# Half of an encoder's input projection as seven block products per pair of tiles, with the mixer's work put in another order

## The chip, the core and the metric

The kernel runs on one core of a Trainium2 chip. The metric is the device time of one execution in microseconds (us); of several runs the median counts. The core has five engines with instruction queues of their own: TensorE (PE, matrix products, results in PSUM banks), VectorE (DVE), ScalarE (ACT), GpSimd (POOL) and SyncE (SP, which here issues transfers). Each works through its queue in order and waits on semaphores for others.

## The reference

Two layers of a hybrid encoder on 1040 rows (16 learned tokens and 1024 inputs) of 1024 channels. Cut to what matters:

```
proj = rmsnorm(x) @ w_in                    # q, k, v, z, b, a, sc_b, sc_c, sc_h
q, k, v = silu(conv3(qkv));  q, k = l2norm(q), l2norm(k)
# per direction, 4 heads of 128, chunks: A = I + strict(beta k k^T * decay)
v_new = u - w @ S;  o = (q*exp(G)) @ S + attn @ v_new
S     = S * exp(G_last) + k_dec^T @ v_new   # the scan over the chunks
o = rmsnorm(o_fwd + o_bwd) * silu(z)
y = sc_b * conv3(sc_c * sc_h)
x = x + concat(o, y) @ w_out
x = x + (silu(h @ w_gate) * (h @ w_up)) @ w_down,   h = rmsnorm(x)
```

A final rmsnorm ends it. u and w come from a triangular solve with A in each chunk.

## The kernel before, in words

Everything lies transposed: 128 channels on the partitions, the 1040 rows along the free axis. Data are fp32; an operand of a dense product is split into a high and a low part (`split_scaled` L176, `wsplit` L124: high part by ACT, L130, low part by POOL or DVE, L131), and each k-step of a dense tile is three matmuls, wh·xh, wh·xl, wl·xh (L157, L158, L159 in `dense`, L146). A tile of the input projection (`inproj`, L290) is 128 output channels: 8 k-steps x 3 matmuls x 3 chunks of 348, 346 and 346 columns, 72 matmuls. In the last layer the gate tiles and the outer factors of the short convolution leave out the 16 tokens and have two chunks of 512.

A layer has four stretches. (1) The mixer's projection, 28 tiles: q 0 to 3, k 4 to 7, v 8 to 11, the gates z 12 to 15 and short convolution 16 to 27 (three tiles for each of four groups). The keys come first, then the queries. Each goes through a convolution of width 3 (`conv`, one ACT and two DVE instructions, L309 and L310), and q and k are normalised (`normalise`, L406) with lengths summed on PE. `k_out` (L418) transposes the keys and copies them by ACT (L426); `chunk_p` (L442) forms key products with their decay; `chunk_a` (L481) those of queries and keys. (2) In each chunk a triangular block is inverted: `substitute` runs 31 DVE steps for each direction, `invert` (L527) puts blocks together on PE and ACT. (3) The scan: `scan_step` (L769) per direction and chunk of 128 rows, nine steps each way. In a step, for four heads: ks = k·S (L792), r by DVE (L795), q·S (L802), its scaled copy qs by ACT (L804), vr (L807), vs by ACT (L810), vn by ACT (L812), then su (L816) for the new state S (DVE, L836) and po (L828, L830) for the output. q·S, vr and po share a PSUM bank of their direction, ks and su another. Once both directions have passed a chunk, `finalize` (L849) normalises its output by ACT and DVE, transposes it on PE (L870) and multiplies by the gate (L871). (4) The output projection (`out_part`, L941) and the feed-forward part, whose products are already done by the scheme of Strassen and Winograd: for four blocks A11 to A22 of weights, sums S1 to S4 of them, and sums T1 to T4 of the data, seven products instead of eight give the four blocks of the result (`prod` L1055, matmuls L1060 to L1062; the down projection L1426 to L1428). The S1 sums of the down projection (`s_under`, `s_sum`, adds at L1151) are made during the gate and up rows.

The order of the work comes from a scheduler that takes the recorded instructions by priority and data: `at_prio` sets the running priority, `mmp` holds a low one for dense matmuls that may fill gaps, `evp` one for evacuations of PSUM, and `jobs`, `jobs2` and `jobs3` are lists from which one small job each is taken after each dense chunk (the end of `dense`). From the values on, all dense tiles take the low priority: 4 value, 4 gate and 12 short-convolution tiles and the lower half of the output projection lie as fill under the second substitution, the inverses and the scan.

Of the kernel before, what the change touches and what calls it, by code (L numbers as in the profile page):

```python
# [15 lines left out]
KT = 8  # L16
# [26 lines left out]
def trunk(ctx: ExitStack, tc: tile.TileContext, xT, w_in, w_ba, w_out, w_gu, w_dn,  # L43
# [188 lines left out]
    for m in range(KT):  # L232
        cs = FULL if m == 0 else [(0, L)]
        for (n0, n1) in cs:
            dma(hv[m][:, n0:n1], xT[m][:, n0:n1])
            if n0 == 0 and m == 0:
                pre[4] = wload(w_in[0, 4], KT)
        for (n0, n1) in cs:
            lasts.append(split_scaled(hv[m][:, n0:n1], par[:, P_N1 + m:P_N1 + m + 1], x[m][0][:, n0:n1], x[m][1][:, n0:n1]))
        if m == 3:  # L240
            pre[5] = wload(w_in[0, 5], KT)
# [37 lines left out]
    hsrc = xT  # L279
    for l in range(DEPTH):  # L280
# [47 lines left out]
        gt = big("P0")  # L328
        wr = gt[:, 3, 0:128].rearrange("p (k m) -> p k m", k=8)
        wb = big("P1", F32R)[:, 0, 0:256].rearrange("p (k m) -> p k m", k=8)  # L330

        def gate_weights():
            dma(wr, w_ba[l])
            act(out=wb[:, :, 0:16], in_=wr, func=AF.Copy)
            tt(out=wb[:, :, 16:32], in0=wr, in1=wb[:, :, 0:16].bitcast(F32), op=ALU.subtract)

        def gates():
            bat = gt[:, 0, :]
# [18 lines left out]
            scr = gt[:, 1, :]  # L357
# [34 lines left out]
            grows = gt[0:72, 2, 0:128]  # L392
# [9 lines left out]


        kq = {"q": big(Y[0][1]), "k": big(Y[0][0])}
        QT, KTt = kq["q"], kq["k"]
        def normalise(dst, l2, r):  # L406

            r4 = row(Y[1] + "f")[:, 0:260]
            act(out=r4, in_=l2[:, 0:260], func=AF.Sqrt, scale=1.0, bias=epsc)
            nc.vector.reciprocal(out=r4, in_=r4)  # L410
            for h in range(H):
                qdma(rnd[r + h].rearrange("(a c) -> a c", a=4), r4.rearrange("(a b) c -> a b c", b=32)[:, h, :])
            for h in range(H):
                bc = c4k("bc")
                qdma(bc, rnd[r + h].partition_broadcast(128))
                tt(out=dst[:, h, :], in0=dst[:, h, :], in1=bc, op=ALU.mult)

        def k_out(c):  # L418
# [4 lines left out]
            for h in range(H):  # L423
                nc.tensor.transpose(ps[0:n, h * 128:(h + 1) * 128], KTt[:, h, s0:s0 + n], ident)
            kt = t2k("kt")
            act(out=kt[0:n].rearrange("p a b -> p (a b)"), in_=ps[0:n], func=AF.Copy)  # L426
            adma(vkd[c, 0:n, 1, :], kt[0:n].rearrange("p a b -> p (a b)"))
# [14 lines left out]
        def chunk_p(c):  # L442
# [8 lines left out]
            for h in range(H):  # L451
                mm(kk[0:n, h, 0:n], KTt[:, h, s0:s0 + n], KTt[:, h, s0:s0 + n], start=True, stop=True)
# [28 lines left out]
        def chunk_a(c):  # L481
# [3 lines left out]
            low(lambda: [mm(qk[0:n, h, 0:n], KTt[:, h, s0:s0 + n], QT[:, h, s0:s0 + n], start=True, stop=True) for h in range(H)])  # L485
# [41 lines left out]
        def invert(d):  # L527
# [19 lines left out]
            def first():  # L547
                for qs in halves:
                    ps = fb(32)
                    low(lambda: [mm(ps[B[s], q - qs.start, :], P_[B[f], q, B[s]], XB[B[f], q, :], start=True, stop=True, skip_group_check=True)  # L550
                                 for q in range(qs.start, qs.stop) for (f, s) in pairs])
# [3 lines left out]
            def second():  # L555
                for qs in halves:
                    ps = fb(32)
                    low(lambda: [mm(ps[B[f], q - qs.start, :], QS[B[s], q, :], P_[B[s], q, B[s]], start=True, stop=True, skip_group_check=True)
                                 for q in range(qs.start, qs.stop) for (f, s) in pairs])
# [3 lines left out]
            def third():  # L563
                f, s = pairs[0]
                fo, so = 32 * (f % 2), 32 * (s % 2)
                for qs in halves:
                    ps = fb(32)
                    low(lambda: [mm(ps[B[s], q - qs.start, :], P_[B[s], q, B[s]], QS[B[s], q, :], start=True, stop=True) for q in range(qs.start, qs.stop)])
# [8 lines left out]
            def fourth(qh):  # L577
                ps = fb(64)
                low(lambda: [mm(ps[S_, q, :], P_[F_, 8 * qh + q, S_], X64[F_, 8 * qh + q, :], start=True, stop=True) for q in range(8)])
                act(out=X64[S_, 8 * qh:8 * qh + 8, :], in_=ps[S_], func=AF.Copy, scale=-1.0)  # L580

            def fifth(qh):
                ps = fb(64)
                low(lambda: [mm(ps[F_, q, :], X64[S_, 8 * qh + q, :], P_[S_, 8 * qh + q, S_], start=True, stop=True) for q in range(8)])
# [6 lines left out]
        def sums(which, q, sq_):  # L591

            if which not in l2s:
                l2s[which] = bank("f")
            for j, (n0, n1) in enumerate([(260 * j, 260 * j + 260) for j in range(4)]):
                mm(l2s[which][32 * j:32 * j + 32, :n1 - n0], sel[:, 3 - q:35 - q], sq_[:, n0:n1], start=(q == 0), stop=(q == 3), skip_group_check=True)
            if q == 3 and which == "k":
                normalise(KTt, l2s["k"], 4)
            elif q == 3:
# [26 lines left out]
        seq = (4, 5, 6, 7, 0, 1, 2, 3)  # L626
        for pos, i in enumerate(seq):
            hh = pos % 4
            if pos == 2:
                gate_weights()  # L630
                evp[0] = base - 60000
            lov[0] = pos > 3
            t = trow()
            late = pos < (2, 1)[l]
            inproj(i, to_row_late(t) if late else to_row(t), pfirst if l == 0 and pos == 1 else None)
            if late:
                tt(out=t, in0=t, in1=rstd, op=ALU.mult)
            dst = (QT if i < 4 else KTt)[:, hh, :]
            if l == 0 and pos == 0:
                pre[seq[2]] = wload(w_in[l, seq[2]], KT)  # L640
            conv(t, dst, P_CV + 3 * i, whi_done[0] if l == 0 and pos == 0 else None)
            if i >= 4:
                lengths("k", hh, dst, t)
            if pos == 2:
                g, negG, nGb, negE, gl, bkd = gates()
            nxt = seq[pos + 1] if pos < 7 else 8
            if nxt not in pre:
                pre[nxt] = wload(w_in[l, nxt], KT)
            if pos == 3:
                jobs.append(None)  # L650
                jobs.extend([lambda c=c: k_out(c) for c in range(9)])
                jobs2.extend([None, None] + [lambda c=c: chunk_p(c) for c in range(9)])

        for hh in range(4):
            lengths("q", hh, QT[:, hh, :], c4k("sq"))
        qs_ = jobs[-4:]
        del jobs[-4:]
        jobs.extend([None, None, None, lambda: [f() for f in qs_]])
        sub_start()
        substitute(0)  # L660

# [3 lines left out]

        def z_tile(m):
            t = trow()
            inproj(12 + m, to_row(t), chunks=ochunks)
            t = t[:, o0:L]
            act(out=t, in_=t, func=AF.Silu)  # L670
            nc.gpsimd.tensor_scalar(out=t, in0=t, scalar1=pcol(P_DN), scalar2=1.0, op0=ALU.mult, op1=ALU.mult)
            dma(szd[m][:, o0:L], t)


        def low(f):

            here = tc.cur_priority
            at_prio(mmp[0])
            f()
            mmp[0] = tc.cur_priority  # L680
            at_prio(here)

        def v_store(i, v, c0):

            ps = pa()
            if c0 == 0:
                low(lambda: nc.tensor.transpose(ps[0:16, 0:128], v[:, 0:16], ident))
                vm = t2k("vm")[0:16, 0, :]
                here = tc.cur_priority
                at_prio(evp[0])  # L690
                nc.vector.tensor_copy(vm, ps[0:16, 0:128])
                evp[0] = tc.cur_priority
                at_prio(here)
                dma(vkd[0, 0:16, 0, i * 128:(i + 1) * 128], vm)
            else:
                vt = v[:, 16 + 128 * (c0 - 1):16 + 128 * (c0 + 3)]
                for c in range(4):
# [871 lines left out]
```

## Time and profile before

| | |
|---|---|
| median of three runs | 2561.62 us (2559.81 to 2562.78) |
| the profiled execution | 2561.09 us |
| its span | 2558.7 us |
| mean granted clock of TensorE | 0.995 |
| TensorE, VectorE, ScalarE, GpSimd busy | 97%, 64%, 42%, 45% of the span |
| layer 0: mixer, feed-forward, down | 0 to 603, 603 to 1073, 1073 to 1256 us |
| layer 1: mixer, feed-forward, down | 1256 to 1872, 1872 to 2316, 2316 to 2499 us |

Rows of the windows read: from and to in us, the length, then for each engine its busy time and (with x) its instructions, the granted clock, the share of busy DMA and GB/s. Rows of the timeline read: start, length, engine, line, operation, output and inputs, shape, count, and in brackets how long the engine had been idle and for what. A group of instructions reads: busy time in all and mean of one in ns, then the idle time just before them and what ended it. A row of waits reads: who waited for whom, us in total, times, the longest.

### The profile page before, as it was taken

Reading aid. Unit: us, or ns where it says so; the run is one execution under the profiler, and the core shown is the slowest. Engines: PE = TensorE matmul, PEld = TensorE weight load, DVE = VectorE, ACT = ScalarE, POOL = GpSimd, SP = SyncE. Lnnn points to the kernel's source line nnn. Section 1 sums busy time; section 2 is a strip of 40 time slices with the busy share of each in tenths; the row PEclk is TensorE's granted clock in tenths of the full one; section 3 lists DMA queues with packets and bytes.
Section 4 is the critical chain, followed back from the end, with each engine's and each line's share of the span. In section 5 each row is a group of like instructions: output and inputs, shape, how many; then the busy total and the mean of one; then the engine's idle time right before and its main releaser. Section 6 shows DMA issues by size and latency. Waiting matters only on the chain. (4 is left out here: it accounts for less than half of the span.)

```text
span 2558.7 us, 45283 instructions
## 1 busy us (share of the span) xinstructions
PE 2494.0 (97%) x17508; PEld 2280.6 (89%) x17508; DVE 1641.7 (64%) x2442; ACT 1070.0 (42%) x2053; POOL 1157.3 (45%) x885
## 2 busy tenths in 40 slices
PE   8999999999999999999999999999989999999998
PEld 6989999998899999999999988998967778887787
DVE  4689233748766666778556882236687776768764
ACT  5664233535233333444445742335442333334444
POOL 1141212525666666655320313123456676675662
PEclk9999999999999999999999999999999999999999
DMA  3444354624432222574224534445343322228641
GB/s 128 139 154 150 119 158 129 200 80 126 136 102 88 89 90 83 195 228 144 92 92 132 164 126 140 133 136 202 118 128 119 112 87 95 91 86 272 190 121 67
DMA packets 199532, 335.28 MB, mean 131 GB/s; under 512 B 23404, under 2 KB 85668, under 8 KB 199316
## 3 DMA queue, kind: packets, MB, share of 16 engines
q1 hardware_dynamic: 171204, 293.84, 35.4%
q10 hardware_dynamic: 25936, 34.19, 4.3%
q0 software_dynamic: 2176, 4.36, 0.5%
q8 instruction: 137, 2.24, 0.4%
q14 instruction: 79, 0.65, 0.1%
HBM read 250.31 MB, written 81.99 MB: 130 GB/s over the span
## 5 line engine op out<-in xcount | busy, mean ns | idle before, releaser
L131 POOL TENSOR_TENSOR wlo<-raw,whi 128x512 fp32r<-128x512 f32 x132 | 175.1, 1329 | 638.0 <-ACT whi L130 523.8
L157 PE MATMUL pacc<-a,whi 128*128 128x346 f32 (+1 forms) x808 | 264.1, 330 | 9.3 <-ACT whi L130 6.4
L159 PE MATMUL pacc<-a,wlo 128*128 128x346 f32 (+1 forms) x808 | 262.5, 326 | 0.6 <-DVE wlo L131 0.4
L157 PE MATMUL pacc<-b,whi 128*128 128x346 f32 (+2 forms) x672 | 233.9, 349 | 1.8 <-ACT b L900 1.8
L159 PE MATMUL pacc<-b,wlo 128*128 128x346 f32 (+2 forms) x672 | 233.0, 348 | 0.1
L158 PE MATMUL pacc<-a,whi 128*128 128x346 f32 (+1 forms) x688 | 225.8, 328 | 0.9 <-DVE a L901 0.9
L130 ACT ACTIVATE whi<-raw 128x512 fp32r<-128x512 f32 x168 | 105.3, 630 | 231.0 <-PE pacc L158 116.5
L158 PE MATMUL pacc<-b,whi 128*128 128x346 f32 (+2 forms) x580 | 200.4, 346 | 0.0
L1043 POOL TENSOR_TENSOR wlo<-rw,whi 128x512 fp32r<-128x512 f32 x92 | 134.6, 1465 | 72.8 <-ACT whi L1042 71.5
L157 PEld LDWEIGHTS pacc<-a,whi 128*128 128x128 f32 x808 | 152.8, 190 | 13.8 <-ACT whi L130 7.9
L159 PEld LDWEIGHTS pacc<-a,wlo 128*128 128x128 f32 x808 | 153.0, 190 | 1.9 <-DVE wlo L131 0.5
L157 PEld LDWEIGHTS pacc<-b,whi 128*128 128x128 f32 x672 | 126.8, 189 | 13.6 <-issue 3.1
L1043 POOL TENSOR_TENSOR a<-rw,a 128x512 fp32r<-128x512 f32 x64 | 105.3, 1646 | 68.2 <-ACT a L1042 65.5
L158 PEld LDWEIGHTS pacc<-a,whi 128*128 128x128 f32 x688 | 130.4, 190 | 5.4 <-issue 2.9
L159 PEld LDWEIGHTS pacc<-b,wlo 128*128 128x128 f32 x672 | 126.6, 189 | 9.2 <-issue 0.8
L1043 POOL TENSOR_TENSOR b<-rw,b 128x512 fp32r<-128x512 f32 x64 | 92.2, 1442 | 84.7 <-ACT b L1042 50.7
L1042 ACT ACTIVATE whi<-rw 128x512 fp32r<-128x512 f32 x92 | 57.8, 630 | 145.3 <-DVE rw L1288 85.0
L158 PEld LDWEIGHTS pacc<-b,whi 128*128 128x128 f32 x580 | 109.5, 189 | 6.9 <-issue 0.4
L1284 DVE TENSOR_TENSOR rw<-rw,rw 128x512 f32<-128x512 f32 x44 | 69.9, 1589 | 46.9 <-POOL wlo L1043 30.9
L1289 DVE TENSOR_TENSOR rw<-raw,rw 128x512 f32<-128x512 f32 x44 | 98.8, 2246 | 1.2
L1043 POOL TENSOR_TENSOR wlo<-raw,whi 128x512 fp32r<-128x512 f32 x50 | 77.9, 1560 | 33.6 <-ACT whi L1042 33.4
L1042 ACT ACTIVATE b<-rw 128x512 fp32r<-128x512 f32 x64 | 40.2, 630 | 123.1 <-PE pacc L1061 35.2
(973 smaller groups left out, 8417.4 us busy)
## 6 DMA issues: line engine op xcount, KB each, us to landing
raw<-in_w_in SPq DMA_DIRECT2D x112, 256.0 KB, 2.9
raw<-in_w_gu SPq DMA_DIRECT2D x104, 256.0 KB, 2.8
rw<-in_w_gu SPq DMA_DIRECT2D x88, 256.0 KB, 2.6
rw<-in_w_dn SPq DMA_DIRECT2D x94, 192.0 KB, 3.0
rec<-vkd SPq DMA_DIRECT2D x61, 256.0 KB, 3.3
raw<-in_w_out SPq DMA_DIRECT2D x48, 256.0 KB, 2.8
b<-ad SPq DMA_DIRECT2D x45, 260.0 KB, 3.0
a<-ad SPq DMA_DIRECT2D x45, 256.0 KB, 3.1
```

The source lines that it names most:

```text
L130: whi_done[0] = act(out=hi, in_=raw[:, 0:kk, :], func=AF.Copy)
L131: (tt if lov[0] else ptt)(out=lo, in0=raw[:, 0:kk, :], in1=hi.bitcast(F32), op=ALU.subtract)
L157: mm(ps[:, :n], wh, xh[:, n0:n1], start=(k == 0), stop=False)
L158: mm(ps[:, :n], wh, xl[:, n0:n1], start=False, stop=False)
L159: mm(ps[:, :n], wl, xh[:, n0:n1], start=False, stop=(k == K - 1))
L1042: act(out=hi, in_=src, func=AF.Copy)
L1043: ptt(out=lo, in0=src, in1=hi.bitcast(F32), op=ALU.subtract)
L1284: tt(out=s1t, in0=A21, in1=A22, op=ALU.add)
L1289: tt(out=A21, in0=A11, in1=A21, op=ALU.subtract)
```

## The change

**Products.** Of the 28 tiles of a layer 14 are taken in pairs: k 4 and 5, 6 and 7; v 8 and 9, 10 and 11; short convolution 16 and 17, 19 and 20, 18 and 21. A pair of tiles by two halves of the 8 k-steps is a 2 x 2 array of blocks, and the two halves of the 1040 columns make the data one; seven block products replace eight. `p_loads` fetches the blocks, `p_op` makes the sums S1 to S4 on DVE and splits them (ACT, POOL) three products ahead, `p_product` does the matmuls (two halves of 260 columns, four k-steps, three matmuls each: 168 in a pair) and adds the results up on DVE. `t_sums` and `t_part` make the data's T1 to T4, once per layer.

```diff
+        PAIRS = [("k", 4, 5), ("k", 6, 7), ("v", 8, 9), ("v", 10, 11), ("sc", 16, 17), ("sc", 19, 20), ("out", 18, 21)]
+        def t_sums(k):
+            w0, w1 = pcol(P_N1 + k), pcol(P_N1 + 4 + k)
+            b11, b12, b21, b22 = (h[:, k, HT * z:HT * z + HT] for h in (hA, hB) for z in (0, 1))
+            act(out=b12, in_=b12, func=AF.Copy, scale=w0)
+            stt(out=b11, in0=b11, scalar=npar[:, k:k + 1], in1=b12, op0=ALU.mult, op1=ALU.add)
...
+        def p_op(n):
+            p, i = divmod(n, 7)
...
+            elif i == 1:
+                r = st["S1"] = rw("ck2")
+                tt(out=r, in0=A21, in1=A22, op=ALU.add)
...
+            act(out=hi, in_=r, func=AF.Copy)
+            ptt(out=lo, in0=r, in1=hi.bitcast(F32), op=ALU.subtract)
...
+        def p_product(n):
...
+                    mm(ps, wh[:, k, :], xh, start=i < 3 and k == 0, stop=False, skip_group_check=True)
+                    mm(ps, wh[:, k, :], xl, start=False, stop=False, skip_group_check=True)
+                    mm(ps, wl[:, k, :], xh, start=False, stop=k == 3, skip_group_check=True)
...
+                if i == 0:
+                    act(out=u0, in_=ps, func=AF.Copy)
+                elif i == 5:
+                    tt(out=g0, in0=ps, in1=r0, op=ALU.mult)
+                else:
+                    to, by = {1: (u1, u0), 2: (g1, u0), 3: (g1, g1), 4: (u1, u1), 6: (u0, u0)}[i]
+                    tt(out=to, in0=ps, in1=by, op=ALU.add)
```

**Order of the mixer.** The four z tiles now come first, then the pairs, then the four query tiles, dense. Key products (`chunk_p`) are jobs under the first two query tiles; the first substitution is recorded behind them. The inverses, `chunk_a` and the second substitution follow at the plain priority, no longer the low one. Keys and queries exchange their buffers, and keys are normalised by pairs of heads.

```diff
+        for n in range(NPR):
+            p_product(n)
+            if n + 3 < NPR:
+                p_op(n + 3)
...
+            if n % 7 == 6:
+                p_rows(n // 7)
...
+        for i in range(4):
+            lov[0] = i < 2
...
+            inproj(i, to_row(tq[i]))
...
+            if i == 1:
+                sub_start()
+                substitute(0)
...
+        for f in invert(0):
+            f()
+        for c in (0, 1, 8, 2, 7, 3, 6, 4, 5):
+            chunk_a(c)
+        substitute(1)
+        for f in invert(1):
+            f()
+        mmp[0] = base + 1000000
...
+        lov[0] = False
+        sc_tile(2)
+        y3 = sc_tile(3)
```

Only these six tiles and the lower half of the output projection are left as fill of low priority. On PE in layer 0 a piece of the scan stood like this before, late in the program (L816, L828 and L807 are products of the scan; L157 to L159 are a dense tile):

```order
L157 MATMUL pacc_3982<-a_3_74,whi_3976 128x348
L816 MATMUL pf_4253<-vv_4251,rec_4246 128x128 x4
L158 MATMUL pacc_3982<-a_4_75,whi_3976 128x348
L828 MATMUL pf_4254<-vv_4251,rec_4246 128x128 x4
L807 MATMUL pb_4256<-vv_4252,P_843 128x128 x4
L159 MATMUL pacc_3982<-a_3_74,wlo_3977 128x348
L157 MATMUL pacc_3982<-a_3_74,whi_3976 128x348
```

Now PE's order in layer 0's scan, from the last rows of the last fill on. L960 is vr, L969 su, L981 po, L945 ks and L955 q·S, all of the forward direction (`pf`):

```order
L157 MATMUL pacc_5938<-a_557_5526,whi_5904 128x346
L158 MATMUL pacc_5938<-a3f_5535,whi_5904 128x346
L159 MATMUL pacc_5938<-a_557_5526,wlo_5905 128x346
L960 MATMUL pf_4671<-vv_4668,P_2669 128x128 x4
L969 MATMUL pf_4670<-vv_4668,rec_4663 128x128 x4
L981 MATMUL pf_4671<-vv_4668,rec_4663 128x128 x4
L945 MATMUL pf_4670<-S_4664,b_140_1000 128x128 x4
L955 MATMUL pf_4671<-S_4664,b_351_2641 128x128 x4
L960 MATMUL pf_4671<-vv_4668,P_2669 128x128 x4
L969 MATMUL pf_4670<-vv_4668,rec_4663 128x128 x4
```

The dense rows between the groups of the scan are gone from here to the output projection: 52 groups follow each other, 45 of the scan and 7 of transposes. The whole scan has nine steps in each direction; this is the fifth to the ninth. Some groups on, the backward direction (`pb`) follows, with the transposes of `finalize` (L1023) ahead of its products:

```order
L1023 MATMUL pa_5116<-ident,b3f_4674 128x128 x4
L960 MATMUL pf_4671<-vv_4668,P_2669 128x128 x4
L981 MATMUL pf_4671<-vv_4668,rec_4663 128x128 x4
L955 MATMUL pb_4673<-S_4665,b_140_1000 128x128 x4
L1023 MATMUL pa_5175<-ident,b3f_4674 128x128 x4
L960 MATMUL pb_4673<-vv_4669,P_2670 128x128 x4
L969 MATMUL pb_4672<-vv_4669,rec_4663 128x128 x4
```

A transpose of the finished chunk stands ahead of L960 on PE, in both directions.

DVE's order around the end of the second pair of keys, in layer 0: L757 and L760 evacuate products, L766 scales, L310 and L311 are the convolution, L446 the normalisation of the first pair, L716 the sum S4 of the next pair's weights:

```order
L757 TENSOR_TENSOR b_143_1017<-pacc_1018,rstd_81 128x260
L757 TENSOR_TENSOR b_143_1017<-pacc_1032,rstd_81 128x260
L760 TENSOR_TENSOR b3f_1016<-pb_1099,b3f_1016 128x260
L760 TENSOR_TENSOR b3f_1016<-pb_1113,b3f_1016 128x260
L766 TENSOR_TENSOR b3f_1016<-b3f_1016,rstd_81 128x520
L310 SCALAR_TENSOR_TENSOR b_140_1000<-b_143_1017,par,b_140_1000 128x1039
L311 SCALAR_TENSOR_TENSOR b_140_1000<-b_143_1017,par,b_140_1000 128x1039
L310 SCALAR_TENSOR_TENSOR b_140_1000<-b3f_1016,par,b_140_1000 128x1039
L446 TENSOR_TENSOR b_140_1000<-b_140_1000,bc_1060 128x1040
L311 SCALAR_TENSOR_TENSOR b_140_1000<-b3f_1016,par,b_140_1000 128x1039
L716 TENSOR_TENSOR rw_1260<-raw_1164,rw_1260 128x512
```

The sum S4, which a product waits for, stands behind the five long rows of the convolution and the normalisation.

**Down sums.** `s_under` now only issues the loads for the S1 sums; the adds stand behind the last operation of the row:

```diff
-            s_under(f)
+            adds = s_under(f)
...
-            tt(out=uv, in0=uv, in1=gv, op=ALU.mult)
+            row_done = tt(out=uv, in0=uv, in1=gv, op=ALU.mult)
+            for to, r, o in adds:
+                after(tt(out=to, in0=r, in1=o, op=ALU.add), row_done if f < FT - 1 else row_before)
+            row_before = row_done
```

355 lines of the change are left out of this document (224 added, 131 removed).

## The prediction

> **What bounds the kernel now.** First the page: how much of the span TensorE works.
>
> ```profile
> span 2558.7 us, 45283 instructions
> PE 2494.0 (97%) x17508; PEld 2280.6 (89%) x17508; DVE 1641.7 (64%) x2442; ACT 1070.0 (42%) x2053; POOL 1157.3 (45%) x885
> ```
>
> TensorE idles 64.7 us in all. So time comes off almost only where matmul work comes off, and every wait that the change adds to PE is paid in full. Next, what a matmul costs, by its columns: a stretch of layer 0's down projection (260 columns) and one of layer 1's feed-forward part (512).
>
> ```profile
> 1100.00:1175.00 75.00, 74.73 (x625) 1.00 0.63 192
> 2050.00:2100.00 50.00, 50.00 (x217) 1.00 0.25 84
> ```
>
> 75.0/625 is 120.0 ns and 50.0/217 is 230.4 ns, start to start; a line through both gives 158.0 ns at the 346.7 columns that a third of 1040 has. Cost goes by columns, so cutting the multiplications pays if PE stays fed. Then the windows in which PE idles in the mixer, which the change rebuilds, and those of the feed-forward part, whose scheme of products the change copies into the mixer.
>
> ```profile
> 100.00:125.00 25.00, 23.58 (x156) 1.00 0.65 208
> 125.00:150.00 25.00, 21.61 (x157) 1.00 0.71 219
> 150.00:175.00 25.00, 24.57 (x167) 1.00 0.45 143
> 475.00:500.00 25.00, 22.31 (x157) 1.00 0.83 287
> 500.00:525.00 25.00, 24.41 (x153) 0.93 0.31 99
> 600.00:625.00 25.00, 19.44 (x142) 0.93 0.31 95
> 1750.00:1775.00 25.00, 22.99 (x121) 0.93 0.79 288
> ```
>
> ```profile
> 600.00:725.00 125.00, 112.19 (x897) 108.94 (x895) 98.39 (x123) 47.30 (x81) 75.19 (x47) 0.99 0.39 124
> 725.00:1075.00 350.00, 344.38 (x2840) 341.42 (x2841) 224.93 (x291) 118.83 (x213) 225.38 (x139) 1.00 0.29 97
> ```
>
> In the second table the third busy column is DVE's. With DVE busy 64% (224.93 of 350) the block products lose 1.6% of PE; in the first 125 us, at 79%, they lose 12.8 us.
>
> **Term 1, the products: -37 us.** A dense tile is 72 matmuls (8 k-steps, 3 products, 3 chunks). Layer 0 gives up 14 tiles, 1008 x 158.0 = 159.3 us; layer 1 gives up 12, 136.5 us, and two that have 48 matmuls of 512, 96 x 230.4 = 22.1 us. Fourteen pairs come in, each 7 products x 4 k-steps x 3 x 2 halves = 168 matmuls of 260 columns: 2352 x 120.0 = 282.2 us. That is 317.9 out, 282.2 in, -35.7; counting one or two fewer matmuls in each window, as those at its edges are counted whole, gives -37. I take -37.
>
> **Term 2, key transposes: -5 us.** The three windows of 100 to 175 lose 1.42, 3.39 and 0.43. What PE waits for there is mostly ScalarE's copy of transposed keys, with no other ready work behind it in PE's order:
>
> ```profile
> PE pa L424 <- ACT kt L426: 2.7, 2, 1.4
> ```
>
> After the change the k_out jobs start three products after the keys' second pair, one product between jobs, so the copy has some 3 us of matmuls over it. All 5.2 us could go; if not, 0.
>
> **Term 3, the down sums: -6 us.** Before, the adds for S1 float among the feed-forward rows, and DVE, which works in order, sits in front of them until their loads land; matmuls wait for the evacuations behind. The first two rows are DVE's waits, the next two PE's in 660 to 715, the last two PE's in 1940 to 1980.
>
> ```profile
>   DMA S<-in_w_dn: 15.4, 7
>   DMA rw<-in_w_dn: 5.9, 4
> ...
> PE pacc L1060 <- DVE a L1326: 1.4, 1, 1.4
> PE pf L1060 <- DVE c L1326: 1.4, 1, 1.4
> ...
> PE pf L1060 <- DVE b L1326: 2.0, 1, 2.0
> PE pa L1060 <- DVE c L1308: 1.2, 1, 1.2
> ```
>
> These four come to 6.0. After, each add stands behind the last operation of its row, a whole row of the loop after its loads were issued, so the loads are hidden. The adds remain and could fall badly: bounds 0 and -8.
>
> **Term 4, the scan's end: +26 us.** Before, 4 value, 4 gate and 12 short-convolution tiles and the lower half of the output projection lie between the scan's steps to the end. After, only 6 tiles and that half are left for it, and in PE's order they run out five steps of nine before the end of each direction. From there PE has 45 groups of state products and 7 of transposes in layer 0, 49 and 7 in layer 1, and nothing else. What one step costs without fill is read from the last backward steps before, which are nearly bare:
>
> ```profile
> 457.23 1.05 PE L792 MATMUL pf<-S,b 128*128 128x128 f32 x8
> 458.12 1.06 PE L802 MATMUL pf<-S,b 128*128 128x128 f32 x8
> ...
> 486.91 1.05 PE L807 MATMUL pb<-vv,P 128*128 128x128 f32 x8
> 488.44 0.73 PE L816 MATMUL pb<-vv,rec 128*128 128x128 f32 x4
> 489.61 0.63 PE L870 MATMUL pa<-ident,b3f 128*128 128x128 f32 x4 [0.44 <-DVE b3f L868]
> 490.07 0.61 PE L816 MATMUL pb<-vv,rec 128*128 128x128 f32 x4
> 492.05 1.16 PE L792 MATMUL pb<-S,b 128*128 128x128 f32 x8 [0.32 <-DVE S L836]
> 493.52 1.05 PE L802 MATMUL pb<-S,b 128*128 128x128 f32 x8
> 495.85 1.16 PE L807 MATMUL pb<-vv,P 128*128 128x128 f32 x8
> ...
> 488.00 1.15 ACT L810 ACTIVATE vv<-pb,bkd 128x128 f32<-128x128 f32 x4
> 494.67 1.12 ACT L804 ACTIVATE qs<-pb,negE 128x128 f32<-128x128 f32 x4
> ...
> 490.88 1.11 DVE L836 SCALAR_TENSOR_TENSOR S<-S,gl,pb 128x128 f32<-128x128 f32 x4
> ```
>
> From one L807 to the next is 8.94 us: the upper price of a bare step. A lower one chains the same rows without what stood between: L807 to L810 1.09, to L816 0.44, four heads of L816 0.89 (the spacing of 457.23 and 458.12), L836 to L792 1.17, L792 to L802 0.89, L802 to L804 1.15, L804 to L807 1.18, in all 6.8. I take 7.4, nearer the lower, since in the row's step dense evacuations stood in DVE's way that will not be there; the finalize transposes (L870) still will. In PE's order layer 0's end has 6 such steps, one in which both directions share (10 groups, 9 us), and some 6.5 us at the hand-over between the directions and at the run-out (estimated): 44.4 + 9 + 6.5 = 59.9, against 45 x 0.89 + 7 x 0.46 (489.61 to 490.07) = 43.3 at PE's own pace. Layer 1 has 5 single and 2 shared: 61.5 against 46.8. The excess is 31.3. What the scan's end loses today goes off it: 2.69 + 0.59 (475 to 525) + 2.01 (1750 to 1775) = 5.3. Net +26; at 6.8 it is +19, at 8.94 +43.
>
> **Term 5, the pairs' feeding: +10 us.** A pair takes PE 20.2 us. What DVE does in it, by rows of before:
>
> ```profile
> L1284 DVE TENSOR_TENSOR rw<-rw,rw 128x512 f32<-128x512 f32 x44 | 69.9, 1589 | 46.9 <-POOL wlo L1043 30.9
> L905 DVE TENSOR_TENSOR a<-pacc,a 128x260 f32<-128x260 f32 x20 | 8.3, 420 | 5.7 <-PE pacc L159 5.7
> L309 DVE SCALAR_TENSOR_TENSOR a<-a,par,a 128x1039 f32<-128x1039 f32 x14 | 19.4, 1386 | 10.3 <-ACT a L308 10.3
> ```
>
> Four sums of weights 4 x 1.59, twelve evacuations 12 x 0.42, four convolution steps 4 x 1.39, and about 0.7 for the half row's scaling (half of such a 1039): 17.7 us, 88% of 20.2. Key pairs add two normalisations. Weight splits have 3 buffers each, and S4's sum stands behind the convolution in DVE's order. The nearest row at that load is 600 to 725. Without its first 25 us (start-up) it loses 7.3 of 100, and 3% if the DMA waits of term 3 are taken out; 725 to 1075 loses 1.6%. On 282 us: 20, 8.5 and 4.5. I take 10, bounds 4 and 20. The Trainium skill, SBUF — State Buffer, section Who interferes with whom, says that a DVE operation with two SBUF inputs and a GpSimd operation that reads SBUF block each other for a whole instruction. The 1589 mean of L1284 fits that; by the rule the four sums could each wait a whole split on POOL, some 8 us for the four, and the term would be nearer 17.
>
> **Term 6, the start: +4 us.** The first evacuation stands at
>
> ```profile
> 29.98 1.37 DVE L301 COPY b<-pacc 128x348 f32<-128x348 f32 x3 [5.78 <-PE pacc L159]
> ```
>
> DVE had been idle 5.78 us before it. Ahead of this copy now stand 12 half-row steps (0.7 each) and five whole-row subtractions (about 1.3), some 15 us, of which the idle 5.78 and DVE's earlier waits for ScalarE's splits hide most. PE meets it only when its banks are full: 0 to 6, taken 4, in layer 0 alone; in layer 1 these sums lie under dense tiles.
>
> Substitution and inverses I cost at nothing: two query tiles, key products and two more dense tiles, about 50 us of PE by the order, lie over the first substitution. If that cover is short, PE idles once in each layer. Normalisation in pairs and the exchanged buffers add no PE work.
>
> **Sum.** -37 - 5 - 6 + 26 + 10 + 4 = -8 on the profiled execution's 2561.1 us (span 2558.7 and 2.4 around it), which is 0.5 below the median of 2561.6: 2554. A measurement of this kernel can tell about 0.2%, 5 us, from no change.
>
> **The rivals.** *Slower: the bare scan.* From row 2679 of the order on, every finalize transpose stands ahead of the next state product on PE and waits for a chain over DVE and ScalarE; the 0.44 before L870 shows it in small. The eleven single steps decide: each 1 us more costs 11 us, and at 8.1 us a step the whole gain is gone; at the measured 8.94, +43 in place of +26 makes 2570; at 11 us it is 2593. For it: 8.94 is measured, not worked out. Against: fill stood in that step's way. Chance 0.30.
>
> *The pairs starve* like the first feed-forward rows, 7%: +20 instead of +10, 2563. Against it: no DMA wait stands in DVE's order there. Chance 0.15.
>
> *The tail is hidden*: the directions run side by side, two steps in 9 us, which is PE's own pace, so that only the 6.5 us of each layer's hand-over, less today's 5.3, is left, +8, and the pairs lose their least: 2561 - 37 - 5 - 8 + 8 + 4 + 4 = 2527. Against it: three forward steps stand alone in the order. Chance 0.10.
>
> *The clock falls in the bare tail.* The granted clock is 0.93 in the windows around short idle (500 to 525, 600 to 625, 1750 to 1775), 1.00 in the other windows above: such gaps already cost about 0.07 x 25 = 1.8 us of clock each. Were PE at half pace through the tail, four groups on each step's path would take 0.89 more, 11 x 3.6 = +39: 2593. The Trainium skill, TensorE: Matmul & The Clock Gate, Part 1, has such a rule: the array is let down to half its clock after an idle window of about 3.4 us. The 0.93 agrees with one window at half pace. Against it: by the rows above no gap inside a step is over some 1.2 us. Chance 0.05.
>
> *The change does not do what it says*: the filler was needed, and what comes off the products goes back one for one into the scan; that is 2561. It lies between the first rival and the forecast, chance 0.05.
>
> **The numbers.** The forecast, 2536 to 2558, has 0.35 and is the likeliest. Faster than by 5 us: 0.30 of the forecast's, 0.10 of the hidden tail, 0.04 of the starved pairs' and 0.03 of the others, 0.47. Within 5: 0.17. Slower: 0.36, the bare scan, the clock and the upper end of the starved pairs. The range reaches from the hidden tail's 2527, a microsecond off, to the 2593 of the clock and of the 11 us step.
>
> **What would show it.** Right: windows of 25 us inside the pairs with some 205 matmuls and PE above 24; no L424 wait; no PE wait behind down sums; and after the last dense matmul of the scan two stretches of some 60 us in each layer in which PE is 70 to 75% busy. Wrong: those stretches at 80 us and more, or windows in the pairs with PE under 23, or PE waiting on the inverses.

## The result and the profile after

The changed kernel takes 2670.5 us (median of four runs, 2665.2 to 2678.8) against 2561.0 before: ratio 1.043, 95% interval 1.041 to 1.044. It is slower by 109 us, where 8 us less were forecast, and lies beyond the range. The profiled execution's span is 2669.6 us. In the experiments below one of four runs took 8097 us (the dense tiles) and one 11626 us (one small job at a time); the ratios leave these two out, the medians do not. The head of the changed kernel's page:

```profile
span 2669.6 us, 46699 instructions
PE 2513.2 (94%) x17892; PEld 2291.0 (86%) x17892; DVE 1786.6 (67%) x2626; ACT 1125.4 (42%) x2148; POOL 1279.9 (48%) x979
```

Two things are to be read from it. TensorE's idle time rose from 64.7 to 156.4 us, 92 us more. And its busy time rose by 19.2 us, though by the forecast's first term some 37 us of matmul work were taken out. The mean granted clock is 0.976 where it was 0.995: over the spans that is 64 against 13 us of clock not granted, about as much as those 19 and 37. So there are two losses, waits and a slower clock. In windows of 50 us all of the added idle time lies in the two mixers: 59 us from 0 to 600 where it was 16, and 52 us in layer 1 (1300 to 1950) where it was 4 (1250 to 1850). Windows of PE show where in them (from and to, length, busy and matmuls, granted clock). The first row is the start before the change. The others are of the changed kernel: the start, the pairs of layer 0, the pairs of layer 1, and the scan's two ends:

```profile
0.00:50.00 50.00, 42.72 (x258) 1.00 0.44 148
...
0.00:50.00 50.00, 38.82 (x234) 0.97 0.47 159
...
100.00:250.00 150.00, 135.67 (x1063) 0.94 0.26 83
1425.00:1575.00 150.00, 131.22 (x1020) 0.94 0.27 84
525.00:605.00 80.00, 59.09 (x393) 0.91 0.41 120
1850.00:1925.00 75.00, 52.65 (x354) 0.89 0.40 121
```

The pairs lose 14 and 19 us to waits and up to 9 us each to the clock (0.06 of 150). The two ends of the scan lose 21 and 22 us to waits and 7 and 8 us to the clock. The middle, substitution and inverses, was costed at nothing and loses too, 12.9 us of waits from 250 to 450 and 5.9 from 1650 to 1700. Two of layer 0's windows:

```profile
300.00:325.00 25.00, 23.43 (x166) 1.00 0.23 79
325.00:350.00 25.00, 19.68 (x114) 0.86 0.35 114
```

Next, some of the longest waits of PE in the whole program. Here L1023 is the transpose of a finalized chunk, L955 q S, L960 vr, L515 the product of queries and keys, L454 and L429 the transposes of keys and values, L628 the sums of lengths, and L302 the evacuation of the first tiles:

```profile
PE pa L1023 <- DVE a3f L1021: 8.5, 5, 5.0
PE pb L960 <- ACT qs L957: 8.2, 10, 2.1
PE pb L515 <- DVE dt L519: 8.1, 3, 4.0
PE pb L955 <- DVE b3f L1011: 6.7, 3, 4.9
...
PE pa L454 <- DVE a L446: 4.3, 1, 4.3
PE pf L628 <- ACT a L655: 4.2, 2, 2.2
PE pf L628 <- ACT b L655: 4.0, 3, 2.0
PE pa L429 <- ACT kt L456: 3.6, 3, 1.5
...
PE pacc L157 <- DVE b L302: 3.4, 1, 3.4
```

Before the change the waits ahead of the same operations were small: 3.9 us ahead of the key transposes (L424), 0.8 ahead of the transposes of finalized chunks (L870) and 0.7 ahead of the sums of lengths (L596). The bare forward step, taken from one L960 to the next in the timeline of layer 0's scan:

```profile
523.88 1.05 PE L960 MATMUL pf<-vv,P 128*128 128x128 f32 x8
...
531.21 1.16 PE L960 MATMUL pf<-vv,P 128*128 128x128 f32 x8 [1.23 <-ACT qs L957]
...
538.64 1.16 PE L960 MATMUL pf<-vv,P 128*128 128x128 f32 x8 [1.23 <-ACT qs L957]
```

It is 7.33 and 7.43 us; the forecast had 7.4. So the price of a bare step was right. The later steps are others. Two backward L960 stand at 566.87 and 584.03, 17.2 us apart, and the chain that ended last passes between them over these pieces (start, length, what):

```profile
572.89 1.98 PE pb L945 x8
...
574.87 0.87 PE pa L1023 x4
...
575.79 2.67 DMA b3f<-od
...
578.62 1.27 POOL b3f L1010
...
579.91 0.70 DVE b3f L1011
...
580.66 2.08 PE pb L955 x8
```

The transposes of one chunk free its buffer; only then the other direction's output of the next chunk is loaded into it, GpSimd subtracts, VectorE adds the product and so frees the PSUM bank, and only then q S of the next step can start. PE idles 4.94 us. Two such chains lie in this one step, since a forward chunk is finalized ahead of the backward one. `finalize` alternates between two halves of one tile, but here they behave as one buffer: the loads of 559.34, 566.45, 575.79 and 583.66 each start within 0.1 us of the end of the transposes of the chunk directly before. The q S that follows lasts 2.08 us where it lasts 1.16 in other steps: the clock is at half there, as the windows of 10 us show. It was so already in the group of 572.89 (1.98 us), behind a wait of 1.70 us:

```profile
570.00:580.00 10.00, 4.02 (x21) 0.82 0.40 131
580.00:590.00 10.00, 8.41 (x36) 0.50 0.14 33
590.00:600.00 10.00, 8.20 (x61) 1.00 0.38 105
```

### The profile page after: what moved, and what is told of

It is laid out like the page before. It is cut to its first block, busy times and chain, and to the rows that moved or that the text cites. A ratio compares the mean times of both kernels' runs of the same rounds, so it can differ in the third digit from the quotient of the medians.

```text
span 2669.6 us, 46699 instructions
## 1 busy us (share of the span) xinstructions
PE 2513.2 (94%) x17892; PEld 2291.0 (86%) x17892; DVE 1786.6 (67%) x2626; ACT 1125.4 (42%) x2148; POOL 1279.9 (48%) x979
## 4 chain that ended last, share of the span: by engine, by line
PE 65%; DVE 18%; issue 5%; DMA 5%; ACT 4%; POOL 2%; ACTq 0%; SPq 0%; DVEq 0%; POOLq 0%
PE pacc L157 4%; PE pacc L159 4%; PE pacc L158 4%; PE pacc L1213 3%; PE pacc L1215 3%; PE pacc L1214 3%; PE pb L1213 2%; PE pb L1214 2%; PE pb L1215 2%; PE pf L1215 2%; PE pf L1214 2%; PE pf L1213 2%; PE pacc L1584 2%; PE pacc L1586 2%; PE pacc L1585 2%
## 5 line engine op out<-in xcount | busy, mean ns | idle before, releaser
L724 POOL TENSOR_TENSOR wlo<-rw,whi 128x512 fp32r<-128x512 f32 x70 | 100.8, 1448 | 149.8 <-ACT whi L723 143.0
L1196 POOL TENSOR_TENSOR wlo<-rw,whi 128x512 fp32r<-128x512 f32 x92 | 130.9, 1423 | 80.0 <-ACT whi L1195 72.7
L157 PE MATMUL pacc<-a,whi 128*128 128x346 f32 (+1 forms) x472 | 154.4, 334 | 11.2 <-ACT whi L130 5.7
L159 PE MATMUL pacc<-a,wlo 128*128 128x346 f32 (+1 forms) x472 | 155.5, 331 | 2.2 <-POOL wlo L131 2.1
L158 PE MATMUL pacc<-a,whi 128*128 128x346 f32 (+1 forms) x394 | 131.8, 335 | 0.6 <-DVE a L178 0.3
L157 PE MATMUL pacc<-b,whi 128*128 128x512 f32 (+2 forms) x352 | 126.6, 361 | 1.8 <-DVE a L757 1.5
L130 ACT ACTIVATE whi<-raw 128x512 fp32r<-128x512 f32 x112 | 69.8, 627 | 134.9 <-PE pacc L158 77.3
L159 PE MATMUL pacc<-b,wlo 128*128 128x512 f32 (+2 forms) x352 | 126.6, 363 | 0.0
L158 PE MATMUL pacc<-b,whi 128*128 128x512 f32 (+2 forms) x300 | 107.8, 360 | 0.0
L157 PEld LDWEIGHTS pacc<-a,whi 128*128 128x128 f32 x472 | 90.8, 194 | 13.9 <-ACT whi L130 5.7
L159 PEld LDWEIGHTS pacc<-a,wlo 128*128 128x128 f32 x472 | 91.2, 193 | 3.1 <-POOL wlo L131 2.7
L1195 ACT ACTIVATE a<-rw 128x512 fp32r<-128x512 f32 x64 | 40.4, 632 | 104.2 <-PE pacc L1214 48.0
L158 PEld LDWEIGHTS pacc<-a,whi 128*128 128x128 f32 x394 | 76.4, 194 | 4.7 <-DVE a L178 2.0
L1394 DVE TENSOR_TENSOR P<-a,P 128x512 fp32r<-128x512 f32 x63 | 60.1, 983 | 22.8 <-ACT P L1393 22.3
```

The costliest lines, as they stand in the source:

```text
L130: whi_done[0] = act(out=hi, in_=raw[:, 0:kk, :], func=AF.Copy)
L157: mm(ps[:, :n], wh, xh[:, n0:n1], start=(k == 0), stop=False)
L158: mm(ps[:, :n], wh, xl[:, n0:n1], start=False, stop=False)
L159: mm(ps[:, :n], wl, xh[:, n0:n1], start=False, stop=(k == K - 1))
L724: ptt(out=lo, in0=r, in1=hi.bitcast(F32), op=ALU.subtract)
L1195: act(out=hi, in_=src, func=AF.Copy)
```

## The experiments

Ratios are to the kernel before, measured alongside; the changed kernel's is 1.043 (1.041 to 1.044). Differences in us are differences of ratios times 2562.

### The down sums alone

```diff
 (kernel before)
-            s_under(f)
+            adds = s_under(f)
+            for to, r, o in adds:
+                after(tt(out=to, in0=r, in1=o, op=ALU.add), row_done if f < FT - 1 else row_before)
```

> The kernel before with the ordered down sums alone. Theory: the adds gave layer 0's gate and up rows the 6 us by which they are shorter after (464.2 against 470.6 us), and the 13 us that layer 1's are longer (456.5 against 443.3) come from something else: this kernel takes 2552 to 2557 us. Rival: the adds cost in layer 1 what they save in layer 0: 2561 us or more.

2555.8 us, ratio 0.997 (0.996 to 0.998): some 7 us faster than before (4 to 10 by the interval), and the only version here that beats both kernels. Layer 0's gate and up rows, from the first to the last of their products; of before first, then of this kernel, with layer 1's:

```profile
603.00:1073.00 470.00, 452.29 (x3703) 1.00 0.32 104
```

```profile
606.00:1070.00 464.00, 450.90 (x3704) 1.00 0.32 105
1870.00:2320.00 450.00, 436.48 (x1863) 0.99 0.32 107
```

The same matmuls take 464 in place of 470 us in layer 0. In layer 1 the 450 us from 1872 to 2322 were 436.51 us busy before; nothing changed. (The expectation's 443.3 us for layer 1 before end at 2316; the last of these products starts at 2322.8, so it is 450.5, and the changed kernel's 456.5 are 6 us longer and not 13.) So the 6 us are layer 0's alone, and what the changed kernel loses in layer 1's rows is not the adds' doing.

### Fill given back

```diff
 (changed kernel)
-        PAIRS = [("k", 4, 5), ("k", 6, 7), ("v", 8, 9), ("v", 10, 11), ("sc", 16, 17), ("sc", 19, 20), ("out", 18, 21)]
+        PAIRS = [("k", 4, 5), ("k", 6, 7), ("v", 8, 9), ("v", 10, 11)]
...
+        while jobs or jobs3:
+            for q in (jobs, jobs3):
+                f = q.pop(0) if q else None
...
+        sc_tile(0)
+        sc_tile(1)
         sc_tile(2)
         y3 = sc_tile(3)
```

> The changed kernel with only the four key and value pairs as block products; the six short-convolution tiles of groups 0 and 1 are dense again and lie with the low priority under the scan. Theory (the bare end of the scan is the greatest single loss, 36 us over PE's own pace in each layer): the end is filled, some 60 us come back, three pairs' products in each layer cost 15 us more of PE and save some 10 to 20 of waits: about 2610 us. Rival (the products' feeding and the new order cost it all, the scan is long whatever fills it): no less than 2660 us.

2622.6 us, ratio 1.024 (1.022 to 1.026): 49 us less, with some 15 us more of matmul work. The small jobs left behind the last pair are emptied there at once, ahead of the queries. The scan of layer 0 and the window in which the small jobs are emptied:

```profile
200.00:225.00 25.00, 15.22 (x80) 0.73 0.75 233
250.00:400.00 150.00, 145.34 (x1604) 0.94 0.37 120
400.00:575.00 175.00, 174.86 (x1284) 1.00 0.48 154
```

The scan, 400 to 575, is full to its end, and layer 1's is too. So the bare end is the largest single loss, as expected; the 2610 us expected were missed by 13. The emptying (first row) is a new loss of this edit.

### The new order with dense tiles

```diff
 (changed kernel)
-        for n in range(NPR):
-            p_product(n)
+        for p, (kind, i1, i2) in enumerate(PAIRS):
...
+            for e, t in enumerate((pst[p]["g"], pst[p]["u"])):
...
+                inproj(i, to_row(t), chunks=ochunks if kind == "out" else FULL)
```

> The changed kernel's order with all fourteen tiles dense and no block products (the data sums T left out too); fill of the scan is as short as in the changed kernel. Theory (the order makes the bare scan, the products lose by their feeding, 20 and 25 us, about what they save, 37): 2660 to 2680 us. Rival (the products are what costs; the order is sound): under 2620 us.

2658.3 us, ratio 1.037 (1.035 to 1.039): 15 us less than the changed kernel, though it has the 37 us of matmul work again. So most of the 109 us is the order's, and the products in their place cost 15 us more than they replaced. Two windows of this kernel:

```profile
0.00:50.00 50.00, 43.96 (x272) 1.00 0.51 175
100.00:200.00 100.00, 98.64 (x649) 1.00 0.34 112
```

Without the data sums the first 50 us are 5 us busier than the 38.82 of the changed kernel, and dense tiles under the same small jobs lose 1.4 of 100 us.

### Four finalize buffers

```diff
 (changed kernel)
-        fin = row(Y[1] + "f")
+        fin = row(Y[1] + "f"), trow()
-            ob = fin[:, 512 * (nfin[0] % 2):512 * (nfin[0] % 2) + 512]
+            i = nfin[0] % 4
+            ob = fin[i % 2][:, 512 * (i // 2):512 * (i // 2) + 512]
...
-            t = trow() if i < 2 else hb[1][:, i, :] if i < 3 else y3
+            t = trow() if i < 1 else hb[1][:, i, :] if i < 3 else y3
```

> The changed kernel with four buffers for the finalized chunks in place of two. Theory: in the bare end the load of a chunk waits for its buffer until the transposes two chunks ahead are done, then GpSimd and VectorE, and only then is the PSUM bank of the next q S free (waits of up to 4.9 us before L955 and L1023, after which the granted clock is 0.5): 8 to 14 us less in each layer, 2642 to 2655 us. Rival: the bare steps alone set the end, 7.4 us each: within 5 us of 2670.

2637.0 us, ratio 1.029 (1.027 to 1.031): 34 us less, 5 more than the theory's best. But this is no clean test. The scheduler put the fill elsewhere: at the scan's end PE is now full, at its beginning it has gaps and waits there for loads (5.9 us ahead of one L960).

```profile
450.00:475.00 25.00, 21.03 (x139) 0.77 0.60 191
...
525.00:600.00 75.00, 75.00 (x556) 1.00 0.34 99
```

So the gain can't be put down to the buffers; the last experiment takes the chain by itself.

### Inverses under the fill again

```diff
 (kernel of "Fill given back")
-        for f in invert(0):
-            f()
...
+        mmp[0] = base + 1000000
+        jobs3.extend(invert(0))
+        sc_tile(0)
+        substitute(1)
+        jobs2.extend([lambda c=c: chunk_a(c) for c in (0, 1, 8, 2, 7, 3, 6, 4, 5)])
+        sc_tile(1)
+        jobs3.extend(invert(1))
```

> The kernel of e2_fill with the inverses and the products of queries and keys as small jobs at the low priority between the dense tiles of the short convolution, and the second substitution behind the first of these groups, as they stood before the change. Theory (the third loss is the order of the mixer's middle: without dense work behind them substitution and inverses leave PE idle, 12.7 us of 200 to 250 and 2.5 and 2.2 of the next two windows in e2_fill's layer 0, with the clock at 0.86 and 0.90): 10 to 20 us less in each layer, 2582 to 2602 us. Rival (what is left in e2_fill is the pairs' feeding and the start): within 8 us of 2622.

2639.1 us, ratio 1.031 (1.029 to 1.033): 18 us more, so both readings failed. (The edit also gives the products of the inverses and of queries and keys the low priority.) The middle did what was expected, the same stretch as above and the scan's end:

```profile
250.00:400.00 150.00, 150.00 (x1675) 1.00 0.32 102
550.00:575.00 25.00, 17.89 (x116) 0.86 0.38 118
```

It is full, 150.00 in place of 145.34 and with the whole clock. But the dense tiles that lie there are missing at the end, which has gaps again: from 250 to 400 PE runs 682 matmuls of dense tiles where the kernel of "Fill given back" runs 555, from 400 to 575 it runs 548 where that one runs 644. Fill is one account for both places.

### Four finalize buffers on top of that

> The kernel of e5_low with four finalize buffers. Theory (the buffers matter in a bare end of the scan alone; in e5_low dense rows lie between the steps): within 5 us of e5_low. Rival (the wait for the buffer costs by itself): some 25 us less than e5_low, as e4_fin4 was 33 less than the changed kernel.

The edit is that of the four buffers. 2620.0 us, ratio 1.023 (1.022 to 1.025): 19 us less than without them. The first theory (within 5 us) failed, and the rival's 25 us are nearer. But the end of the kernel it is built on had gaps, so the first theory's condition wasn't met, and again the fill moved: the scan's end is full (25.00 of 25 us in each window from 525 to 600), and from 475 to 500 PE is busy 13.95 of 25 us. What the buffers gave by themselves is open here too.

### Pairs without sums of weights

```diff
 (changed kernel)
-                r = st["S1"] = rw("ck2")
-                tt(out=r, in0=A21, in1=A22, op=ALU.add)
+                r = st["S1"] = A22
 (S2, S3, S4 likewise)
```

> The changed kernel without the four sums of weights of each pair: raw blocks are split in the place of S1 to S4. Theory (VectorE's load in the pairs makes the 20 and 25 us that PE loses there; the sums are a third of that load): 15 to 30 us less, 2640 to 2655 us. Rival (the pairs lose on chains of transposes and lengths that share a PSUM bank, whatever VectorE does): 2662 to 2672 us.

The four sums are left out, so the blocks multiplied are raw. 2666.6 us, ratio 1.042 (1.040 to 1.044): no different from the changed kernel. Its pairs:

```profile
100.00:250.00 150.00, 136.45 (x1081) 0.95 0.29 90
```

That is 136.45 where the changed kernel has 135.67. So the sums do not set the length of the pairs. They are less of VectorE's work than the expectation's third: 20.8 of the 95.3 us that it is busy from 100 to 250 in the changed kernel. And another wait on VectorE took their place: without the sums the key transposes (L454) wait 4.5 us for normalised keys (L446) in this window, where they waited 0.2, and 7.2 in layer 1's, where they waited 4.3.

### One small job at a time

```diff
 (changed kernel)
+                jobs.append(None)
...
-            for q in (jobs, jobs2, jobs3):
-                f = q.pop(0) if q else None
-                if f is not None:
-                    f()
+            q = jobs or jobs3
+            f = q.pop(0) if q else None
+            if f is not None:
+                f()
```

> The changed kernel with one small job behind each block product in place of up to three (lengths and value stores first, then key stores), and lengths one product later. Theory (e6_nosums showed that the pairs do not lose on VectorE's sums; what is left are the chains of transposes and their copies that share one PSUM bank, 6 us at 191 to 200 alone, the lengths' sums, 3 us, and the clock of 0.88 and 0.91 behind them): 8 to 12 us less in each layer, 2646 to 2655 us. Rival (the waits move to other products, as the evacuations set the pace): within 6 us of 2670.

2649.2 us, ratio 1.034 (1.032 to 1.037): 22 us less, as the theory had it. The sums of lengths also come one product later. From 175 to 250 us:

```profile
175.00:200.00 25.00, 25.00 (x212) 1.00 0.34 107
200.00:225.00 25.00, 25.00 (x212) 1.00 0.33 107
225.00:250.00 25.00, 25.00 (x211) 1.00 0.56 181
```

212 matmuls in 25 us, 118 ns each, with the clock at 1.00: fed like this, the products run at the price that the forecast gave them. In the changed kernel a key store and a value store came behind the same product; both transpose into the one PSUM bank `pa`, and each waits for ScalarE's copy of the other. These waits for copies are gone here. What is left of the pairs' idle time, 9.6 us from 100 to 250 and 10.3 from 1425 to 1575, lies mostly ahead of block products and sums of lengths, for split weights (L723, L724), emptied banks (L760) and squares (L655).

### Values ahead of keys

```diff
 (kernel of "Fill given back")
-        PAIRS = [("k", 4, 5), ("k", 6, 7), ("v", 8, 9), ("v", 10, 11)]
+        PAIRS = [("v", 8, 9), ("v", 10, 11), ("k", 4, 5), ("k", 6, 7)]
...
-            if i == 1:
+            if i == 2:
                 sub_start()
                 substitute(0)
```

> The kernel of e2_fill with the value pairs ahead of the key pairs, so that no small jobs have to be emptied between the pairs and the query tiles (key stores and key products lie under the query tiles, the first substitution one tile later). Theory (e2_fill lost 9.8 us of PE in 200 to 225, with the clock at 0.73, on that emptying): 10 to 16 us less in each layer, 2592 to 2604 us. Rival (the later substitution takes back what the emptying gave): 2615 to 2635 us.

2609.0 us, ratio 1.018 (1.016 to 1.020): 15 us less than the kernel it is built on, the theory's direction, but short of its 20 to 32. Key stores and key products lie under the query tiles here. The emptying at once is gone, and the first pairs, behind which no lengths are summed, run full:

```profile
100.00:125.00 25.00, 25.00 (x213) 1.00 0.28 84
125.00:150.00 25.00, 24.96 (x209) 1.00 0.26 76
200.00:225.00 25.00, 23.43 (x173) 1.00 0.55 192
```

It is the fastest kernel here with block products in the mixer, and still 46 us slower than the kernel before.

### Finalize without the other direction

```diff
 (changed kernel)
-                dma(ob[0:n], od[c])
-                ptt(out=o, in0=o, in1=qs[0:n], op=ALU.subtract)
-                tt(out=ob[0:n], in0=pof, in1=ob[0:n], op=ALU.add)
+                tt(out=ob[0:n], in0=pof, in1=qs[0:n].rearrange("p h e -> p (h e)"), op=ALU.subtract)
```

> The changed kernel whose finalize leaves out the other direction's output: no load of it and no subtraction on GpSimd, so VectorE frees the PSUM bank as soon as the chunk's own product is there. PE's order in the scan's end stays bare (45 groups of the scan and 7 of transposes). Theory (in the bare end the load behind the transposes, 2.7 us, then GpSimd's 1.3 us stand ahead of the next q S; the waits of 4.9 us and the clock of 0.5 behind them go): the step of 17.2 us becomes some 8, 8 to 16 us less in each layer, 2640 to 2655 us. Rival (another link of the same chain takes over, ScalarE's squares or the state): within 6 us of 2670.

The outputs of the two directions are not added. 2651.7 us, ratio 1.036 (1.034 to 1.037): 18 us less, inside the theory's range. The scan's end is as bare as in the changed kernel and lasts 66 us in layer 0 (526.4 to 592.4). Backward steps of layer 0 in this kernel's timeline:

```profile
562.62 1.16 PE L960 MATMUL pb<-vv,P 128*128 128x128 f32 x8 [0.46 <-ACT qs L957]
...
569.07 0.63 PE L1021 MATMUL pa<-ident,b3f 128*128 128x128 f32 x4 [1.13 <-DVE b3f L1019]
571.08 2.07 PE L955 MATMUL pb<-S,b 128*128 128x128 f32 x8 [1.38 <-DVE b3f L1009]
574.39 2.07 PE L960 MATMUL pb<-vv,P 128*128 128x128 f32 x8 [1.23 <-ACT qs L957]
...
583.49 1.06 PE L960 MATMUL pb<-vv,P 128*128 128x128 f32 x8
```

The longest step is 11.8 us where it was 17.2 (some 8 were expected), and the wait ahead of L955 1.38 where it was 4.94. So the load and GpSimd's subtraction stood in the chain of the steps, and together cost some 9 us in each layer. The half clock is not gone with them: the groups of 571.08 and 574.39 last 2.07 us, and no wait in this end is over 1.51.

## Why the prediction was wrong, point by point

**The products** were right: 118 ns each where nothing disturbs them, 120.0 were taken. **The down sums** came out at -7 for a forecast of -6, but that is partly luck: the forecast took 2.8 us from layer 0's waits and 3.2 from layer 1's, and layer 0 gave 6.4 (464.1 in place of 470.5 us) and layer 1 nothing. **The start** was right: 42.72 us busy of the first 50 before, 38.82 after, -3.9 for a forecast of 4, and the dense version of the same order has 43.96. The new wait is the one expected, 3.4 us for a late evacuation (L302).

**The key transposes** (term 2, -5) failed in the step that counted "one product between jobs". From the three lists up to three jobs follow one product, and key stores share their bank with the value stores. The waits moved from L424 to L454 and L429 and did not go. The longest of them, 4.3 us in layer 1, has another cause, which the term left out: the keys were not yet normalised (L446).

**The pairs' feeding** (term 5, +10) was mis-sized, and the step that failed is its measure, VectorE's load. The term reckoned 88% and read the loss from feed-forward windows with a similar load. The loss was 14 and 19 us of idle PE, and up to 9 us of clock in each layer, and it does not go with that load: from 100 to 250 VectorE was busy 64% (95.3 of 150 us), at which the forecast's rows lose 1.6%, and PE idled 9.5%; with values first VectorE was busy 74% (36.8 of 50 us from 100 to 150) and PE ran full. Without the sums nothing changed; with the jobs spread 22 us came back. The windows chosen as nearest had no transposes in them, and the value pairs that run full have the same sums and evacuations, but no lengths and no normalisation. So the loss belongs to what the keys bring, of which the transposes behind one product are shown and the rest was not taken apart. The rule on the port that VectorE and GpSimd share, from the Trainium skill (SBUF — State Buffer, Who interferes with whom), would have added 7 us; since leaving out two-input sums did not shorten the pairs, no run here shows that it costs this stage. (The 8 us for four waits are also more than four of the splits on GpSimd, 1.33 to 1.65 us each before.)

**The scan's end** (term 4, +26) had its single step right, 7.4 us, and its steps with finalize wrong: `finalize` entered them by its transposes on PE alone, with no wait for its load. The 7.4 was a choice between 6.8 and 8.94. The upper price of 8.94 was read from a single short step that stood 17.5 us behind the one before it (L807 at 469.38 and 486.91); there the load of the chunk had started at 484.07, 2.8 us before the step, and in the step of 17.2 us it starts 8.9 us after the step's beginning. With the steps close together the chain of transposes, load, GpSimd, VectorE and q S is longer than the step: the transposes of successive chunks start 7.1 to 9.6 us apart (558.66, 565.75, 574.66, 582.53, 592.13). The bare ends last some 79 us (from 523.9) and 84 us (from 1839.2) where 59.9 and 61.5 were counted; against PE's own pace of 43.3 and 46.8 that is an excess of 73 in place of 31.3. Without the load and the subtraction layer 0's end still lasts 66 us, so they are not all of the excess. The rival of the bare scan named the mechanism, "waits for a chain over DVE and ScalarE", without the load, and stopped at 11 us a step.

**Substitution and inverses** at nothing: the sentence that failed is "about 50 us of PE by the order, lie over the first substitution". That cover was counted for one substitution and not for the products of queries and keys (L515, 8.1 us) or the inverses behind it. The experiments with the low priority showed that cover here and cover at the end are the same dense tiles (682 matmuls for 555 here, 548 for 644 there). What the forecast should have counted is the fill of the whole stretch: 20 tiles and the half projection before, 6 and the half after.

**The clock** was a rival at 0.05, on the argument that no gap is over some 1.2 us. The gaps of up to 5 us made that false. In the windows around them the granted clock is 0.50 to 0.9. The Trainium skill (TensorE: Matmul & The Clock Gate, Part 1) lets the array down to half its clock after an idle window of about 3.4 us. The trace agrees in part: behind the idle 4.94 us groups of eight passes last 2.07 us where they last 1.06 to 1.16. But half pace came without such a gap too: behind 1.70 us in the changed kernel (572.89), and without the other direction behind gaps of 1.13 and 1.38 us with only four transposes between them (569.07, 571.08). So short gaps do not exclude it where little work lies between them; in the bare forward steps, with gaps of 0.51 and 1.23 us in 7.4, the groups stayed at 1.06 to 1.26. How much of the 51 us of clock would come back by itself was not measured, and it does not follow the idle time: "Fill given back" idles 43 us less than the changed kernel at a clock of 0.977, "Inverses under the fill again" 25 us less at 0.982, values first 49 us less at 0.986.

Together the forecast missed by 117 us. The scan's ends are 42 us of it, the pairs with their clock up to 41 (51 for 10), the waits of the middle 19 that were counted as nothing; the rest, some 15, was not taken apart. The forecast's own signs of being wrong came about: one end at over 80 us, and windows of 25 us in the pairs with PE under 23 (20.71 from 175 to 200).

What stays open: the changed kernel's layer 1 takes 456.5 us from its first gate and up product to its last, where before took 450.5, which the adds alone don't do; and in the version with values first the rest of the 46 us lies in several windows, of which no single one was taken apart.

## What to carry to other kernels

Dense work of low priority is an account from which every latency-bound stretch is paid; before moving tiles out of it, sum the waits of all the stretches that draw on it, not of the nearest one. The price of a bare step must come from a place where the whole loop, loads and buffers included, runs at that pace. And where PE has had little idle time, price the clock beside the gaps: here 92 us of added idle time came with 51 us of clock.

## What the runs showed of the hardware that was not expected

Around an idle gap of 4.94 us in a scan the granted clock was 0.50 for some 10 us (580 to 590 in the changed kernel, eight passes in 2.07 us), and over the kernel the mean fell from 0.995 to 0.976, 51 us of clock for 92 us of added idle time. Half pace needs no gap of that length: in the kernel without the other direction eight passes took 2.07 us behind gaps of 1.13 and 1.38 us, between which PE had only four transposes. Block products of 260 columns ran at 118 ns, no slower than in the feed-forward part (120.0 in the stretch read there), with VectorE at work on sums, evacuations and convolutions beside them.
